# Layer 1's feed-forward in the form of layer 2: half blocks' products, down sums by row block, and the next layer's modulation on VectorE

## The chip, the cores and the metric

One core of a Trainium2 chip runs the whole kernel. The metric is the device time of one execution in microseconds (us). The core has five engines with an instruction list each, which each works through in its own order: TensorE (PE, matmuls), VectorE (DVE), ScalarE (ACT), GpSimd (POOL) and SyncE (SP, which here only issues DMA transfers; GpSimd issues some too).

## What is computed

Two layers of a backbone with 1024 latent and 256 context tokens of width 1024. The part that the change touches is the second half of layer 1 and the start of layer 2. `g2`, `sh2` and their like come from a modulation, a product of SiLU(c) with a 1024 x 6144 matrix per layer.

```
for i in range(DEPTH):                                  # 2 layers
    mod = (s_lat @ w_mod[i] + b_mod[i])[:, None, :]     # latents; mod_c the same from s_ctx, for the context
    sh1, sc1, g1, sh2, sc2, g2 = jnp.split(mod, 6, axis=-1)
    h = rms_norm(x, norm_mix[i]) * (1.0 + sc1) + sh1
    y, yc = token_mixers(h, hc, ...)
    x = x + g1 * y
    h = rms_norm(x, norm_ffn[i]) * (1.0 + sc2) + sh2
    x = x + g2 * swiglu(h, w_gate[i], w_up[i], w_down[i])   # 1024 -> 2816 -> 1024
    if need_ctx_out:                                    # layer 1 alone: the same for the context, xc
        ...
return rms_norm(x, final_norm)
def swiglu(h, w_gate, w_up, w_down):
    return (jax.nn.silu(h @ w_gate) * (h @ w_up)) @ w_down
```

All is float32. A product of two float32 operands is made from three matmuls of rounded operands: high by high, high by low and low by high part. Layer 1 is `l == 0` in the code, layer 2 `l == 1`.

## The kernel before

Tokens lie along the free axis, features on the 128 partitions: `x[k]` holds 128 features of 1280 tokens, latents in the blocks `B0` and `B1` of 512 and the context in `BC` of 256. `split` (lines 230 to 235) makes the two parts of a weight: ScalarE rounds the high one (L232), VectorE subtracts for the low one (L234), in a pool `wx` of eight buffers that also holds other tiles. A weight arrives in one of two buffers `wr` by a DMA of SyncE.

**Layer 1's FFN** is `ffn`. For each of 22 groups `f` of 128 hidden features it loads a column block of gate and up and a row block of down, and for each of the three token blocks it makes gate and up (`pg`, `pu`, 24 matmuls each, L441), the hidden value `a`, its parts `ah` and `al`, and then for each of the 8 output row blocks `m` three matmuls into `pd` (L1156), which VectorE adds at once into `x[m]` with the gate as factor (L1157). So VectorE takes 528 results out of PSUM. `last_norm` is the context's norm, which runs beside the first group. The squares for the next norm come with the last `f` (`add`), and layer 2's norm (`norm_block`) runs from there, block by block, beside layer 2's first projections, as the jobs in `pending`.

**Layer 2's modulation** is made meanwhile by `modulation_aside`: twelve units of 512 columns, each the sum of eight row blocks of `w_mod` times a scalar per partition, for latents and context (`v`). GpSimd multiplies and adds (L345, L346, `macc`), SyncE loads (`wm`), VectorE transposes and sums each unit (L351, L352), and four matmuls and an addition at the end turn it into `modT`. A merge draws two of its steps for three of `ffn`'s.

**Layer 2's FFN** has another form already. `out_proj` writes x to DRAM (`xmD`), since the norm then takes its place. `gates_seven` takes the 1024 latents as two halves of tokens and the 1024 features as two halves of rows, pairs the groups `f` and makes each 2 x 2 block product from seven products of half blocks in place of eight, with sums and differences of operands: `token_sums` makes those of the tokens once (`t1` to `t4`), `weights` those of the weights on GpSimd. The first four jobs (`early`) have their first two products drawn ahead of the token sums, as these need the norm and time. The hidden value goes to DRAM, `aD`. Then `down_blocks` loads the hidden features of 512 tokens (`hidden`: a load through GpSimd's queue and a split each, `ha`), and per output row block `m` three weights (1024, 1024 and 768 rows) give 66 matmuls into one `pd` (L1379), which VectorE adds to `xm` (L1398).

**What sets the order.** The program is written as above and given to a scheduler that works with a model of the engines (`schedule_with_timeline_sim`): it may put an engine's instructions in another order than they are written in, while the buffers of a pool go to the tiles in the order of the code. Each engine then runs its list as it stands, and an instruction that waits holds all behind it on its engine.

Of the kernel before, what the change touches and what calls it, by code (L numbers as in the profile page):

```python
# [11 lines left out]
F32 = mybir.dt.float32  # L12
# [75 lines left out]
def hybrid_layers(ctx: ExitStack, tc: tile.TileContext, A, K, out):  # L88
# [105 lines left out]
    xmD = [dr.tile([128, T], F32, name=f"xmD{k}") for k in range(KD)]  # L194
    aD = [dr.tile([128, T], F32, name=f"aD{f}") for f in range(NF)]
# [132 lines left out]

    def halves(t):
        return [t[:, 0:512], t[:, 512:1024]]  # L330

    def modulation_aside(l, u0, u1, part, sums, select):
        nu = u1 - u0
        pv4 = part[:, 0:32 * nu].rearrange("p (v b) -> p v b", v=2)
        for u in range(u0, u1):
            acc = sums()
            for k in range(KD):
                r = t_p("wm")[:, 0:512]
                SY.dma_start(r, A["w_mod"][l, 128 * k:128 * k + 128, 512 * u:512 * u + 512])
                for v in range(2):  # L340
                    if k == 0:
                        G.tensor_scalar(acc[v], r, sT[:, k, v:v + 1], None, ALU.mult)
                        continue
                    t = t_ev("mp")
                    G.tensor_scalar(t, r, sT[:, k, v:v + 1], None, ALU.mult)  # L345
                    G.tensor_tensor(acc[v], acc[v], t, ALU.add)  # L346
                if k % 2:
                    yield
            for v in range(2):
                t = t_ev("mtr")  # L350
                V.transpose(t, acc[v])  # L351
                V.tensor_reduce(pv4[:, v, 16 * (u - u0):16 * (u - u0) + 16], t.rearrange("p (b c) -> p b c", c=32),  # L352
                                axis=AX.X, op=ALU.add)
            yield
        sel = select()
        G.memset(sel, 0.0)
        for g in range(4):
            r = slice(32 * g, 32 * g + 32)
            V.tensor_copy(rev(sel[r], 0, [[160, 4], [1, 32]]), ident[r, r].unsqueeze(1).to_broadcast([32, 4, 32]))
        tp = p_c("modt")  # L360
        for q in range(4):
            PE.matmul(tp[:, 0:8 * nu], sel[:, 128 * q:128 * q + 128],
                      part[:, 0:32 * nu].rearrange("p (m q) -> p q m", q=4)[:, q], start=(q == 0), stop=(q == 3))
        V.tensor_tensor(modT[l][:, :, 4 * u0:4 * u1], tp[:, 0:8 * nu].rearrange("p (v j) -> p v j", v=2),
                        bmT[:, 48 * l + 4 * u0:48 * l + 4 * u1].unsqueeze(1).to_broadcast([128, 2, 4 * nu]), ALU.add)
        for w in range(2):
            if u0 <= 6 * w + 3 < u1:
                mod_vectors(l, w)
        yield


# [116 lines left out]
    def gla(l, hh, hl, ctx_out, before, given):  # L488
# [8 lines left out]
        def gproj(items, put, with_ctx, given=()):  # L497
            given = list(given)
            w = given + [None] * (len(items) - len(given))
            for blk in blks:  # L500
# [570 lines left out]
    def out_proj(l, blks):  # L1071
# [9 lines left out]
        def part(grp):  # L1081
# [6 lines left out]
            for m in range(KD):  # L1088
                w = wcols(A["w_out"][l], 128 * m)
                for o, n in grp:  # L1090
# [6 lines left out]
                    if len(blks) == 2:  # L1097
                        G.dma_start(xmD[m][:, o:o + n], x[m][:, o:o + n])
# [3 lines left out]
        def norms():  # L1102
            for blk in blks[:-1]:
                rs = block_rstd(ss, blk)
                yield
                r = rs()
                for k in range(KD):
                    xv, pool = x[k][:, blk[0]:blk[0] + blk[1]], k % 2 == 1
                    if len(blks) == 2:
                        scaled(l, xv, r, k, yh, yl, blk)  # L1110
                    else:
                        modulate(l, 1, xv, r[:, :blk[1]], k, yh, yl, blk, pool)
                    yield
        run(merge(part(blks[-1:]), norms(), 1, 2))
        rs = block_rstd(ss, blks[-1])
        if len(blks) == 2:
# [483 lines left out]
```

## Time and profile before

| | us |
|---|---|
| median of 3 runs (range) | 3234.38 (3233.16 to 3243.77) |
| the profiled execution | 3235.02 |
| its span, first to last instruction | 3233.2 |
| layer 1's FFN, first matmul to the last start of a down matmul | 886.7 to 1826.0 |
| layer 2's half-block products | 2514.8 to 2960.5 |
| layer 2's down sums and the final norm | 2962.1 to 3233.2 |

The span's mean granted clock of TensorE is 0.972 of full speed. A row that counts instructions as x528 has 528 of them in the group; a window's row gives for each engine the busy time and, in brackets, the number of instructions. Matmuls overlap in TensorE, so the distance between two starts is the price of one, and not the duration that its row shows.

### The profile page before, as it was taken

The page shows a single profiled execution, that of the slowest core. Times are in us where ns is not written, and L with a number is a line of the kernel's source. Part 1 is how long each engine was busy: PE and PEld are TensorE (multiplying, and loading weights), DVE is VectorE, ACT ScalarE, POOL GpSimd, SP SyncE. Part 2 cuts the span into 40 slices and gives each one's busy share as a digit, 9 for nine tenths or more (in the row PEclk, how much of TensorE's full clock was granted, in tenths as well). Part 3 has the DMA queues.
Part 4 walks back from the last instruction along what each step waited for, and adds up shares of the span by engine and source line. Part 5 has one row for each costly group of instructions (what it writes and reads, how often), then busy time and mean ns, then how long its engine had stood idle before and what let it go on. Part 6 is the DMA issues. An engine that isn't in the chain of part 4 may idle for free.

```text
span 3233.2 us, 50611 instructions
## 1 busy us (share of the span) xinstructions
PE 3067.4 (95%) x19726; PEld 2613.5 (81%) x19726; DVE 1726.4 (53%) x3431; ACT 1044.3 (32%) x1976; POOL 1087.8 (34%) x938
## 2 busy tenths in 40 slices
PE   7998999889999999999999899999989899999998
PEld 5887877677878888888888789887868688887877
DVE  3255444566675666666555724545766644444342
ACT  4332223455321111111111432224664444333231
POOL 1011020230189888887000101110411376655010
PEclk8999999999999999999999898999999999999999
DMA  7233455764312222222111223356555232225452
GB/s 251 84 125 104 126 160 156 209 186 155 92 62 72 82 79 82 79 82 66 40 40 38 76 66 98 95 155 184 148 172 171 69 101 79 79 85 170 143 187 80
DMA packets 371543, 365.80 MB, mean 113 GB/s; under 512 B 65100, under 2 KB 297512, under 8 KB 371304
## 3 DMA queue, kind: packets, MB, share of 16 engines
q1 hardware_dynamic: 358296, 318.79, 32.6%
q0 software_dynamic: 11856, 39.59, 3.8%
q10 hardware_dynamic: 1152, 4.19, 0.3%
q8 instruction: 155, 2.54, 0.3%
q14 instruction: 84, 0.69, 0.1%
HBM read 285.86 MB, written 76.64 MB: 112 GB/s over the span
## 4 chain that ended last, share of the span: by engine, by line
PE 72%; DMA 5%; DVE 4%; issue 3%; POOL 2%; ACT 1%; SPq 0%; DVEq 0%; ACTq 0%; POOLq 0%
PE q L1286 10%; PE pg L441 9%; PE pd L1156 9%; PE pu L441 9%; PE pd L1379 7%; PE op L441 6%; PE nqk L441 4%; PE ptp L849 3%; PE swp L448 2%; PE gp L441 1%; PE nao L863 1%; PE swo L863 1%; DMA wm<-in_w_mod_dram 1%; PE nvp L448 1%; PE gvp L448 1%
## 5 line engine op out<-in xcount | busy, mean ns | idle before, releaser
L1157 DVE SCALAR_TENSOR_TENSOR x<-pd,modT,x 128x512 f32<-128x512 f32 (+1 forms) x528 | 317.9, 655 | 195.0 <-PE pd L1156 192.9
L345 POOL TENSOR_SCALAR mp<-wm,sT 128x512 f32<-128x512 f32 x168 | 283.8, 1701 | 42.0 <-DVE mpart L352 35.9
L1286 PE MATMUL q<-yh,ws 128*128 128x512 f32 (+1 forms) x1056 | 282.9, 356 | 4.4 <-DVE us L1346 2.6
L1379 PE MATMUL pd<-ha,wdh 128*128 128x512 f32 (+1 forms) x748 | 225.2, 384 | 5.3 <-ACT ha L1170 2.2
L346 POOL TENSOR_TENSOR macc<-macc,mp 128x512 f32<-128x512 f32 x168 | 224.1, 1360 | 0.0
L830 ACT ACTIVATE P<-P,m 128x640 f32<-128x640 f32 (+2 forms) x216 | 167.2, 775 | 137.4 <-DVE m L826 131.4
L1286 PEld LDWEIGHTS q<-yh,ws 128*128 128x128 f32 x1056 | 183.3, 190 | 34.8 <-ACT ws L1170 5.6
L234 DVE TENSOR_TENSOR wcl<-wr,wch 128x1024 fp32r<-128x1024 f32 x98 | 140.7, 1435 | 124.1 <-ACT wch L232 122.5
L441 PE MATMUL pg<-yh,wch 128*128 128x512 f32 (+1 forms) x528 | 187.9, 356 | 1.0 <-ACT a L1146 1.0
L441 PE MATMUL pg<-yl,wch 128*128 128x512 f32 (+1 forms) x528 | 187.9, 356 | 0.0
L441 PE MATMUL pg<-yh,wcl 128*128 128x512 f32 (+1 forms) x528 | 187.4, 355 | 0.0
L441 PE MATMUL pu<-yl,wch 128*128 128x512 f32 (+1 forms) x528 | 187.1, 354 | 0.0
L441 PE MATMUL pu<-yh,wcl 128*128 128x512 f32 (+1 forms) x528 | 187.0, 354 | 0.0
L441 PE MATMUL pu<-yh,wch 128*128 128x512 f32 (+1 forms) x528 | 186.9, 354 | 0.0
L232 ACT ACTIVATE wch<-wr 128x1024 fp32r<-128x1024 f32 x100 | 106.0, 1060 | 245.3 <-PE pg L441 89.9
L1156 PE MATMUL pd<-al,wdh 128*128 128x512 f32 (+1 forms) x528 | 184.9, 357 | 0.0
L1156 PE MATMUL pd<-ah,wdl 128*128 128x512 f32 (+1 forms) x528 | 184.7, 357 | 0.0
L1286 PE MATMUL q<-yl,ws 128*128 128x512 f32 (+1 forms) x528 | 173.8, 356 | 0.4 <-DVE yl L1189 0.4
L1379 PEld LDWEIGHTS pd<-ha,wdh 128*128 128x128 f32 x748 | 139.9, 192 | 35.2 <-ACT ha L1170 3.8
L849 PE MATMUL ptp<-ident,P 128*128 128x128 f32 x984 | 144.5, 286 | 10.0 <-DVE pT L855 7.8
L1156 PE MATMUL pd<-ah,wdh 128*128 128x512 f32 (+1 forms) x528 | 148.6, 356 | 0.3 <-ACT ah L1149 0.3
L1379 PE MATMUL pd<-ha,wdl 128*128 128x512 f32 (+1 forms) x374 | 143.5, 384 | 0.8 <-DVE wdl L234 0.7
(351 smaller groups left out, 7809.9 us busy)
## 6 DMA issues: line engine op xcount, KB each, us to landing
wm<-in_w_mod_dram SPq DMA_DIRECT2D x96, 256.0 KB
wr<-in_w_gate_dram SPq DMA_DIRECT2D x46, 512.0 KB
wr<-in_w_up_dram SPq DMA_DIRECT2D x46, 512.0 KB
wm<-in_w_mod_dram POOLq DMA_DIRECT2D x32, 512.0 KB, 4.7
wr<-in_w_out_dram SPq DMA_DIRECT2D x32, 512.0 KB
wr<-in_w_down_dram SPq DMA_DIRECT2D x32, 512.0 KB
k<-naD SPq DMA_DIRECT2D x48, 320.0 KB
gm<-in_const_nam_dram SPq DMA_DIRECT2D x24, 576.0 KB
```

The lines of the kernel that those rows point to most:

```text
L232: S.activation(h, raw, AF.Copy)
L234: engine.tensor_tensor(l, raw, h.bitcast(F32), ALU.subtract)
L345: G.tensor_scalar(t, r, sT[:, k, v:v + 1], None, ALU.mult)
L346: G.tensor_tensor(acc[v], acc[v], t, ALU.add)
L441: PE.matmul(pt[:, :n], a[:, k, :], b[k][:, o:o + n], start=(k == 0 and i == 0), stop=(k == KD - 1 and i == 2))
L448: PE.matmul(pt[:, :n], a[k][:, t * 128:(t + 1) * 128], b[:, k % 2, c0:c0 + n], start=(k == 0 and i == 0), stop=(k == KD - 1 and i == 2))
L830: exps[:] = [S.activation(P, P, AF.Exp, bias=m[:, i:i + 1], scale=-1.0, accum_out=sums[:, i:i + 1])]
L849: line[:] = [PE.transpose(tp[:, (cc * 2 + i) * 128:(cc * 2 + i + 1) * 128], pr[i][:, (c + cc) * 128:(c + cc + 1) * 128], ident)]
L1156: PE.matmul(pd[:, :n], w[:, m * 128:(m + 1) * 128], b[:, :n], start=(i == 0), stop=(i == 2))
L1157: V.scalar_tensor_tensor(x[m][:, o:o + n], pd[:, :n], modT[l][:, v, 40 + m:41 + m], x[m][:, o:o + n], ALU.mult, ALU.add)
L1286: PE.matmul(bank[:, n * c:n * c + n], wv[p], v, start=(start and k == 0 and q == 0), stop=(k == 3 and q == 2), skip_group_check=not start)
L1379: PE.matmul(pt[:, 0:n], w[i][:, f - f0, :], hs[f][b][:, c0:c0 + n], start=(f == 0 and q == 0), stop=(f == NF - 1 and q == 2))
```

## The change

It does five things.

1. `ffn` and `modulation_aside` go. `out_proj` writes x to DRAM in layer 1 too, context included, and puts the latents' norm in x's place by `scaled`.
2. `gates_seven` takes the context along (`ctx_too`): with a job's first products the weights of the halves `a11` and `a12` also multiply the context's normed tokens (`context`), and once more at the job's end with `a21` and `a22`; `context_done` makes the hidden value. `early` is three there, and the token sums `t2` lie elsewhere, since the context's tokens now fill the place that layer 2 uses.
3. `down_next` makes the down sums by row block for the two latent blocks and then for the context. Each block of sums is added to `xm`, written to DRAM for layer 2, squared on ScalarE and added to `ss` on VectorE.
4. The modulation moves from beside the gates to beside the down sums of the latents (`modulation_behind`, four steps for a row block) and from GpSimd to VectorE, which now multiplies and adds in one instruction; the first four units are made for latents and context, the other eight for one of them. Its loads go through GpSimd's queue into the pool `ev` of three buffers.
5. Layer 2's norm of the latents runs beside the context's down sums (`norms`, a step for every third draw), that of the context after them (`last_norm`), and layer 2's first projections take the blocks in the order B0, B1, BC.

```diff
@@ out_proj @@
-                    if len(blks) == 2:
-                        G.dma_start(xmD[m][:, o:o + n], x[m][:, o:o + n])
+                    G.dma_start(xmD[m][:, o:o + n], x[m][:, o:o + n])
...
@@ gates_seven @@
         def first_products(j, pa, pb):
-            product(0, pa, True)
-            product(1, pb, True)
+            w = product(0, pa, True)
+            if ctx_too:
+                bank = p_b("qc")
+                context(w, 0, bank)
+            w = product(1, pb, True)
+            if ctx_too:
+                context(w, 1, bank)
+                context_done(j, 0, bank)
...
+        def context(w, half, bank):
+            for k in range(4):
+                for q, (p, y) in enumerate(((0, yh), (0, yl), (1, yh))):
+                    PE.matmul(bank[:, 0:C], w[k][p], y[4 * half + k][:, T:N], start=(half == 0 and k == 0 and q == 0),
+                              stop=(half == 1 and k == 3 and q == 2))
...
@@ new: modulation_behind(l) @@
+        for u in range(12):
+            acc = t_x("macc", F32)
+            nv = 2 if u < 4 else 1
+            for k in range(KD):
+                r = t_ev("wm")
+                G.dma_start(r, A["w_mod"][l, 128 * k:128 * k + 128, 512 * u:512 * u + 512])
+                for v in range(nv):
+                    if k == 0:
+                        V.tensor_scalar(acc[:, v], r, sT[:, k, v:v + 1], None, ALU.mult)
+                    else:
+                        V.scalar_tensor_tensor(acc[:, v], r, sT[:, k, v:v + 1], acc[:, v], ALU.mult, ALU.add)
+                if k % 2:
+                    yield
+            for v in range(nv):
+                t = t_ev("mtr")
+                V.transpose(t, acc[:, v])
+                V.tensor_reduce(pv4[:, v, 16 * u:16 * u + 16], t.rearrange("p (b c) -> p b c", c=32),
+                                axis=AX.X, op=ALU.add)
+            yield
...
@@ new: down_next(l) @@
+        def sums(m, hs, n, pt):
+            for f0 in range(0, NF, KD):
+                nf = min(KD, NF - f0)
+                r = t_raw("wr", [128, KD, 128])
+                SY.dma_start(r[:, 0:nf], A["w_down"][l][128 * f0:128 * (f0 + nf), 128 * m:128 * m + 128]
+                             .rearrange("(k p) f -> p k f", p=128))
+                w = split(r[:, 0:nf], "wd", [128, nf, 128])
+                for f in range(f0, f0 + nf):
+                    for q, (i, b) in enumerate(((0, 0), (0, 1), (1, 0))):
+                        PE.matmul(pt[:, 0:n], w[i][:, f - f0, :], hs[f][b], start=(f == 0 and q == 0),
+                                  stop=(f == NF - 1 and q == 2))
...
+            for m in range(KD):
+                SY.dma_start(xs[m], xmD[m][:, o:o + n])
+                pt = either(p_a, p_b, "pd")
+                sums(m, hs, n, pt)
+                V.scalar_tensor_tensor(xs[m], pt[:, 0:n], modT[l][:, v, 40 + m:41 + m], xs[m], ALU.mult, ALU.add)
+                if blk != BC:
+                    SY.dma_start(xD[l + 1][:, m, o:o + n], xs[m])
+                if m == 0:
+                    S.activation(ss, xs[m], AF.Square)
+                else:
+                    sq = t_ev("sq")[:, 0:n]
+                    S.activation(sq, xs[m], AF.Square)
+                    V.tensor_tensor(ss, ss, sq, ALU.add)
+                for _ in range(4):
+                    next(aside, None)
...
@@ the driver @@
-        x, hh, hl, last_norm = out_proj(l, blks)
-        if not ctx_out:
-            gates_seven(l, x, hh, hl, last_norm)
+        x, hh, hl, rs = out_proj(l, blks)
+        gates_seven(l, x, hh, hl, rs, ctx_out)
+        if ctx_out:
+            hh, hl, last_norm = down_next(l)
+        else:
```

In the change's order of VectorE's instructions a row is line, operation, output and inputs, and the tile's size; "x2" stands for two alike in a row. The first piece is from layer 1's FFN in the kernel before: `pd` is a product of down, `macc` the modulation, `pu` the up product, `wcl` and `wch` the parts of a weight.

```order
L1157 SCALAR_TENSOR_TENSOR x_8278<-pd_9744,modT_113,x_8278 128x256
L1157 SCALAR_TENSOR_TENSOR x_8279<-pd_9749,modT_113,x_8279 128x256
L351 STREAM_TRANSPOSE mtr_10799<-macc_10429 128x512
L352 TENSOR_REDUCE mpart_9293<-mtr_10799 128x16
L351 STREAM_TRANSPOSE mtr_10802<-macc_10429 128x512
L1147 TENSOR_TENSOR a_9804<-a_9804,pu_9779 128x512
L352 TENSOR_REDUCE mpart_9293<-mtr_10802 128x16
L1150 TENSOR_TENSOR al_9808<-a_9804,ah_9807 128x512
L234 TENSOR_TENSOR wcl_9958<-wr_9954,wch_9956 128x1024
L1157 SCALAR_TENSOR_TENSOR x_8272<-pd_9811,modT_113,x_8272 128x512
```

Additions into x follow the matmuls one by one, with the modulation's transposes between them. Now VectorE's list in the down stage of layer 1, from the middle of the third latent row block on (lines are those of the changed kernel): `pd_14148` is the sum of that block (block 2, counting from 0), `wdl_14275` the low half of the first weights of block 3.

```order
L1331 SCALAR_TENSOR_TENSOR macc_14122<-wm_14139,sT,macc_14122 128x512
L1331 SCALAR_TENSOR_TENSOR macc_14122<-wm_14143,sT,macc_14122 128x512 x2
L1383 SCALAR_TENSOR_TENSOR xm_13896<-pd_14148,modT_113,xm_13896 128x512
L1391 TENSOR_TENSOR ss_13900<-ss_13900,sq_14235 128x512
L1331 SCALAR_TENSOR_TENSOR macc_14122<-wm_14238,sT,macc_14122 128x512 x2
L1331 SCALAR_TENSOR_TENSOR macc_14122<-wm_14242,sT,macc_14122 128x512 x2
L1336 STREAM_TRANSPOSE mtr_14246<-macc_14122 128x512
L1336 STREAM_TRANSPOSE mtr_14249<-macc_14122 128x512
L1337 TENSOR_REDUCE mpart_13990<-mtr_14246 128x16
L1337 TENSOR_REDUCE mpart_13990<-mtr_14249 128x16
L1329 TENSOR_SCALAR macc_14252<-wm_14253,sT 128x512 x2
L234 TENSOR_TENSOR wdl_14275<-wr_14271,wdh_14273 128x1024
```

There is one addition for a whole row block, and eleven more of VectorE's instructions stand between it and the next block's first weights. The second place is TensorE at the end of layer 1's FFN in the kernel before: `gp` is layer 2's first projection, over the context (`yh`, `yl` are its normed tokens), `ssb` and `rsb` the next block's norm, `pd` the last products of down.

```order
L441 MATMUL gp_17186<-yl_8271,wch_17182 128x256
L441 MATMUL gp_17186<-yh_8263,wcl_17184 128x256
L393 MATMUL ssb_16946<-ones,ss_16888 128x1 x4
L404 MATMUL rsb_17013<-ident,rbc_17011 128x128 x4
L1156 MATMUL pd_17056<-ah_17007,wdh_16653 128x512
L1156 MATMUL pd_17056<-al_17008,wdh_16653 128x512
L1156 MATMUL pd_17056<-ah_17007,wdl_16655 128x512
L1156 MATMUL pd_17071<-ah_17007,wdh_16653 128x512
```

There layer 2's projection over the context is drawn in among the last down products, and the norm's matmuls stand between. Now the end of the context's down sums: `hc` is the context's hidden value, `hh` and `hl` the latents' normed tokens.

```order
L1366 MATMUL pd_16746<-hc_15973,wdh_16809 128x256 x2
L1366 MATMUL pd_16746<-hc_15973,wdl_16811 128x256
L1366 MATMUL pd_16746<-hc_15973,wdh_16809 128x256 x2
L1366 MATMUL pd_16746<-hc_15973,wdl_16811 128x256
L397 MATMUL gp_16854<-hh_15982,wch_16850 128x512
L397 MATMUL gp_16854<-hl_15990,wch_16850 128x512
L397 MATMUL gp_16854<-hh_15982,wcl_16852 128x512
L397 MATMUL gp_16854<-hh_15983,wch_16850 128x512
```

The projection, over latents now, follows the last down product directly, with no matmul of a norm between.

## Rows read from the trace of the kernel before

**Rows 1.** The page's busy line: engine, busy us, share of the span, instructions.

```profile
PE 3067.4 (95%) x19726; PEld 2613.5 (81%) x19726; DVE 1726.4 (53%) x3431; ACT 1044.3 (32%) x1976; POOL 1087.8 (34%) x938
```

**Rows 2.** Windows by stage: length, busy us PE PEld DVE ACT POOL, clock, DMA share, GB/s.

```profile
886.50:1810.00 923.50, 916.64 (x4782) 789.16 (x4781) 566.25 (x835) 158.10 (x235) 554.09 (x372) 1.00 0.20 64
2514.60:2961.50 446.90, 431.04 (x2126) 364.93 (x2124) 218.68 (x267) 180.10 (x310) 261.16 (x177) 0.98 0.27 84
2961.50:3233.20 271.70, 256.96 (x1186) 211.48 (x1186) 108.14 (x141) 79.59 (x122) 34.31 (x53) 0.96 0.47 150
```

**Rows 3.** Timeline of TensorE: start, duration, engine, line, operation, output and inputs.

```profile
1744.57 0.39 PE L441 MATMUL pg<-yh,wch 128*128 128x512 f32 x1
...
1750.01 0.39 PE L441 MATMUL pu<-yh,wch 128*128 128x512 f32 x1
...
1760.89 0.28 PE L441 MATMUL pg<-yh,wch 128*128 128x256 f32 x1
...
1763.04 0.28 PE L441 MATMUL pg<-yh,wch 128*128 128x256 f32 x1
```

**Rows 4.** Tiles pg, pd: count, ns least/median/most, first and last start, forms.

```profile
L441 PE MATMUL pg<-yh,wch x528: 277/389/792, 886.7 to 1791.2; 128*128 128x512 f32 x110, 128*128 128x256 f32 x66
...
L1156 PE MATMUL pd<-ah,wdl x528: 278/389/628, 907.9 to 1826.0; 128*128 128x512 f32 x110, 128*128 128x256 f32 x66
```

**Rows 5.** Tile q, the half blocks' products of layer 2.

```profile
L1286 PE MATMUL q<-yh,ws x1056: 277/389/632, 2514.8 to 2957.8; 128*128 128x512 f32 x111, 128*128 128x256 f32 x65
...
L1286 PE MATMUL q<-t,ws x528: 388/389/797, 2547.3 to 2960.5; 128*128 128x512 f32 x176
```

**Rows 6.** Timeline of ScalarE: copies of a job's first product, fourteen jobs apart.

```profile
2617.72 0.60 ACT L1306 ACTIVATE p<-q 128x512 f32<-128x512 f32 x1 [0.94 <-PE q L1286]
...
2886.80 0.60 ACT L1306 ACTIVATE p<-q 128x512 f32<-128x512 f32 x1 [2.04 <-PE q L1286]
```

**Rows 7.** Windows within layer 2's half-block stage (first) and its down stage.

```profile
2550.00:2570.00 20.00, 14.26 (x62) 11.42 (x61) 14.94 (x25) 6.73 (x11) 6.64 (x5) 0.78 0.26 79
2961.00:2980.00 19.00, 15.49 (x49) 10.83 (x50) 12.15 (x13) 7.33 (x13) 13.43 (x16) 0.82 0.72 245
3000.00:3050.00 50.00, 50.00 (x222) 41.41 (x221) 16.02 (x16) 10.81 (x11) 0.00 (x0) 1.00 0.42 126
3110.00:3130.00 20.00, 17.78 (x66) 13.90 (x66) 9.28 (x13) 5.05 (x9) 2.18 (x3) 0.83 0.88 280
```

**Rows 8.** Groups by line and form on VectorE: busy us, mean ns, idle before.

```profile
L234 DVE TENSOR_TENSOR wdl<-wr,wdh 128x1024 fp32r<-128x1024 f32 x32 | 39.2, 1224 | 50.6 <-ACT wdh L232 49.7
...
L383 DVE TENSOR_TENSOR ss<-ss,sq 128x512 f32<-128x512 f32 x42 | 28.8, 686 | 1.0
...
L351 DVE STREAM_TRANSPOSE mtr<-macc 128x512 f32<-128x512 f32 x24 | 16.8, 701 | 0.0
...
L352 DVE TENSOR_REDUCE mpart<-mtr 128x16 f32<-128x512 f32 x24 | 16.0, 677 | 0.4
...
L419 DVE TENSOR_SCALAR nt<-nt,av,modT 128x512 f32<-128x512 f32 x16 | 13.4, 840 | 0.4 <-ACT yh L418 0.3
...
L1398 DVE SCALAR_TENSOR_TENSOR xm<-pd,modT,xm 128x512 f32<-128x512 f32 x15 | 11.2, 750 | 28.2 <-PE pd L1379 27.9 <-DMA xm<-xmD 0.3
```

**Rows 9.** Timeline of ScalarE and VectorE near the start of layer 2's half-block stage.

```profile
2510.68 0.63 ACT L382 ACTIVATE sq<-x 128x512 f32<-128x512 f32 x1 [0.20 <-ACT ws L1170]
...
2527.91 2.74 DVE L1187 SCALAR_TENSOR_TENSOR x<-x,av,rs 128x512 f32<-128x512 f32 x4 [1.45 <-ACT rs L406]
```

**Rows 10.** DMA issues of GpSimd's queue: count, KB each, median us to landing.

```profile
ar<-aD POOLq DMA_DIRECT2D x44, 256.0 KB, 5.1
...
xmD<-x POOLq DMA_DIRECT2D x16, 256.0 KB, 2.4
```

**Rows 11.** Timeline of ScalarE in layer 2's down stage: two high halves of weights.

```profile
3004.24 1.06 ACT L232 ACTIVATE wdh<-wr 128x1024 fp32r<-128x1024 f32 x1 [1.69 <-DVE wdl L234]
3007.87 1.06 ACT L232 ACTIVATE wdh<-wr 128x1024 fp32r<-128x1024 f32 x1 [2.56 <-DMA wr<-in_w_down_dram]
```

More of the change, by code (lines that the diff above doesn't have):

```diff
@@ L325, in modulation @@
             yield
[L329 to L369, printed above, removed]
     def square_sums(x, blks):
@@ L499, in gproj @@
             w = given + [None] * (len(items) - len(given))
-            for blk in blks:
+            for blk in blks if l == 0 else (B0, B1, BC):
                 for i, (c0, ctx_too) in enumerate(items):
@@ L1209, in token_sums @@
         for k in range(4):
-            t1, v22 = half(x[k], 0), half(x[k + 4], 1)
+            t1, v22, v21 = half(x[k], 0), half(x[k + 4], 1), half(x[k + 4], 0)
             V.tensor_tensor(t1, v22, t1, ALU.subtract)
+            if ctx_too:
+                V.tensor_tensor(v21, v21, t1, ALU.subtract)
+                ops["t2"][k] = whole(t_s("t2", F32R) if k else t_x("t2"))
+                parts(t1, b2[k], ops["t2"][k])
+                continue
             j = 2 * k
@@ L1273, in gates_seven, with take @@
         ready = [next(feed) for _ in range(3)]
-        def product(i, bank, start):
-            w, b = ready.pop(0), ops[order[i]]
+        def take():
+            w = ready.pop(0)
             new = next(feed, None)
@@ L1279, in product @@
                 ready.append(new)
+            return [[t.rearrange("p (k f) -> p k f", f=128)[:, k] for t in w] for k in range(4)]
+        def product(i, bank, start):
+            w, b = take(), ops[order[i]]
             for k in range(4):
-                wv = [t.rearrange("p (k f) -> p k f", f=128)[:, k] for t in w]
                 for q, (p, m) in enumerate(((0, 0), (0, 1), (1, 0))):
@@ L1322, in gates_seven @@
         next(sums)
[L1323 removed]
+        if early == 4:
+            held[3] = first_products(3, p_b("q1"), p_b("q2"))
         run(sums)
@@ L1347, in gates_seven, with modulation_behind @@
             done(j, 1)
-            product(6, pd, False)
+            if ctx_too:
+                bank = p_b("qc")
+                context(take(), 0, bank)
+            w = product(6, pd, False)
+            if ctx_too:
+                context(w, 1, bank)
+                context_done(j, 1, bank)
             V.tensor_tensor(result(j, 2), u2, pd, ALU.add)
             done(j, 2)
+    def modulation_behind(l):
+        part = wk.tile([128, 7, 64], F32, tag="sx", name=nm("mpart"), bufs=2).rearrange("p a b -> p (a b)")[:, 0:384]
+        V.memset(part, 0.0)
+        pv4 = part.rearrange("p (v b) -> p v b", v=2)
+        for u in range(12):
[17 more added lines that the diff above has]
+            yield
+        sel = t_ev("sel")
+        V.memset(sel, 0.0)
+        for g in range(4):
+            r = slice(32 * g, 32 * g + 32)
+            V.tensor_copy(rev(sel[r], 0, [[160, 4], [1, 32]]), ident[r, r].unsqueeze(1).to_broadcast([32, 4, 32]))
+        tp = p_c("modt")
+        for q in range(4):
+            PE.matmul(tp[:, 0:96], sel[:, 128 * q:128 * q + 128],
+                      part.rearrange("p (m q) -> p q m", q=4)[:, q], start=(q == 0), stop=(q == 3))
+        V.tensor_tensor(modT[l][:, :, 0:48], tp[:, 0:96].rearrange("p (v j) -> p v j", v=2),
+                        bmT[:, 48 * l:48 * l + 48].unsqueeze(1).to_broadcast([128, 2, 48]), ALU.add)
+        for w in range(2):
+            mod_vectors(l, w)
+        yield
@@ L1354, in down_blocks, with norms_first @@
+    def norms_first(gen):
+        for i, _ in enumerate(gen):
+            yield
+            yield
+            yield
     def down_blocks(l, gain):
```

160 lines of the change are left out of this document (80 added, 80 removed).

## The prediction

> **What bounds the kernel now.** I read the page's busy line first: TensorE is busy for 95% of the span [rows 1]. A busy share says nothing about a stage, so the windows by stage come next [rows 2]: in layer 1's FFN TensorE is busy for 916.6 of 923.5 us at a granted clock of 1.00, VectorE for 566 and GpSimd for 554. That stage ends when TensorE has issued its matmuls; nothing else sets it. The timeline gives the price of one: 24 matmuls of 512 columns start between 1744.57 and 1750.01, which is 5.44 / 24 = 0.2267 us each, and 18 of 256 columns between 1760.89 and 1763.04, 0.12 each [rows 3]. One f of 22 is 144 matmuls of 512 columns and 72 of 256: 144 x 0.2267 + 72 x 0.12 = 41.28, in all 908. The stage runs from 886.7 to 1826.0, 939.3 us [rows 4]; the 31 beyond 908 are its start, and its end with layer 2's first projections drawn into it.
>
> Layer 2 already runs the form that layer 1 gets, so its rows carry the estimate: half blocks' products from 2514.8 to 2960.5 [rows 5], at 19.22 us a job once they run (14 jobs from 2617.72 to 2886.80 by ScalarE's copy of a job's first product) [rows 6], then the down sums by row block.
>
> **The change, part by part.** Times are set against the profiled execution's 3235.0 us, 0.6 above the median of the three runs.
>
> 1. *Seven products for eight.* Gate and up over the latents take 2 x 2 x 24 x 22 = 2112 matmuls of 512 columns before and 22 x 7 x 12 = 1848 after; the context's and the down sums' numbers stay. 264 x 0.2267 = **-59.9 us**. The order of instructions has exactly 264 fewer matmuls.
>
> 2. *VectorE's additions into x and the modulation's place.* 528 evictions of down products become 24, and most of the 554 us of GpSimd work there goes. In the stage of before TensorE waits for neither [rows 2], so this gives nothing back: **0**.
>
> 3. *Both ends of the stage.* Layer 2's half-block stage needs 22 x 19.22 = 422.8 and lasts 445.7: 23 us are lost, most of them at its start while VectorE builds the token sums (busy 14.9 of the 20 us from 2550, TensorE 14.3) [rows 7]. Layer 1 has the context's products of three jobs in hand there (24 x 0.12 = 2.9 us a job), so I take 19. At the end TensorE goes straight from the context's last down product to projections whose norm is done (the order's second place): 2. Together 21 against 31: **-10** (-18 to +4, as the cover holds or not).
>
> 4. *Down sums begin.* In layer 2 the 19 us from 2961 hold 49 matmuls where 3000 to 3050 shows 4.44 a us, or 84: 35 x 0.2267 = 7.9 us [rows 7]. With the modulation's first loads among the `ha` loads: **+10** (5 to 15).
>
> 5. *Ten waits between row blocks.* This is what the change adds. VectorE's order in the down stage (first place of the order) puts, after block 2's eviction `xm<-pd_14148`, the `ss` addition, four `macc`, two transposes, two reduces and two `macc` of the next unit ahead of `wdl_14275`, the low half of block 3's first weights. VectorE runs its list in order, the eviction needs block 2's last matmul, and TensorE's list has block 3 directly behind block 2: after two matmuls it stands until that split is done. Number the 16 latent row blocks 0 to 15. The same holds from 1 to 2, 2 to 3, 3 to 4, 5 to 6, 6 to 7, 7 to 8, 10 to 11, 11 to 12, 12 to 13 and 13 to 14. At the other five changes the weights stand ahead. In layer 2's down of before nothing stands there, hence 4.44 matmuls a us.
>
> Prices: eviction 0.75, addition 0.69, transpose 0.70, reduce 0.68, weight split 1.22 [rows 8]; square on ScalarE 0.63 and `macc` 0.69 (four `x<-x,av,rs`, same kind and size, in 2.74) [rows 9]. With two handovers the addition ends 2.2 after the last matmul. The `macc` that starts a unit has one tensor operand: the nearest row, L419, reads 0.84, taken beside work of GpSimd [rows 8], so I take 0.6. The loads of w_mod now leave GpSimd's queue into three buffers, so several are issued only when a `macc` frees one. A 256 KB transfer of that queue takes 2.4 us (`xmD`, little else under way) or 5.1 (`ar`, five at once) [rows 10]. One to three are under way here: I take 3.5 and keep both ends.
>
> - 2 to 3: 2.2, four `macc` 5.0; the next load is issued there and lands at 8.5 (transposes and reduces, 2.8, fit beside); two starts 9.7; split **10.9**.
> - 1 to 2: two evictions, two transposes, addition 3.6; load 7.1; two starts, two `macc` 9.7; split **10.9**.
> - 3 to 4: 2.2; eight `macc`, the last four behind loads, 8.5; next load 12.0; two starts, split **14.4**.
> - 5 to 6: load issued at 1.5 lands at 5.0; `macc`, split **6.9**.
> - 6 to 7, 10 to 11, 11 to 12: no load in the way, **4.8** each.
> - 7 to 8: seven `ha` splits of the next half stand there too, 11.0, and a load: **12.5**.
> - 12 to 13: two `macc`, load 6.4, start, `macc`, split **8.9**.
> - 13 to 14: four `macc` (two behind loads) 7.2, load 9.9, start, `macc`, split **12.6**.
>
> Sum **+92**; with loads of 2.4 us it is 81, with 5.1 it is 108.
>
> What a rule would add: the Trainium skill's page "SBUF — State Buffer", section "SBUF: two separate sides", says that a DMA issued from GpSimd's queue waits for its descriptors while VectorE runs an instruction that takes both ports, a tensor_scalar among them, and gives 620 ns alone against 3100 beside one. That speaks against moving these loads and this work together. The 5.1 us of `ar`, issued between VectorE's splits, lean that way [rows 10]. By that rule alone, 2.5 us on the seven waits with a load would make the sum 110.
>
> 6. *The clock after a stop.* From 2961 to 2980 TensorE was idle for 3.5 us, but 7.9 us of matmuls are missing, at a granted clock of 0.82; from 3110 to 3130 idle 2.2, missing 23 x 0.2267 = 5.2, at 0.83; 2550 to 2570 shows 0.78 [rows 7]. So a stop costs 3 to 4.4 us beyond itself, spent at the lower of two levels. No row shows ten in turn: nothing as the one end, 44 as the other; I take 3 each: **+30**.
>
> 7. *The context's down sums.* Ideal 8 blocks of 66 x 0.12 = 7.9 us. Each block needs three weight loads through two buffers: in layer 2 a split that waits for its load starts 3.6 us after the one before [rows 11]; with its own 1.06 and the low half's 1.22 a buffer turns in 5.9, so there is a load every 2.95 us, and as the third is three quarters of the others, 8.5 a block: 8 x 0.6 = 5. VectorE has, per block, 3.4 of splits (2.75 x 1.22), 3.0 of the next norm (two parts of two instructions at 0.75) and 0.9 of sums at half size, 7.3, and stays below. Two broadcasts of the next norm's root, each a wait of TensorE for VectorE and ScalarE, add 4: **+9** (3 to 18).
>
> Sum: -59.9 + 0 - 10 + 10 + 92 + 30 + 9 = +71, so 3235 + 71 = **3306 us**.
>
> **Rivals.** *The stops are covered* (faster). Nine of the ten waits rest on where VectorE's weight split stands; if the split were in truth ready before the block ends, as in layer 2 [rows 7], terms 5 and 6 fall: 3235 - 51 = 3184. It decides from the mean stop: ten stops of 5.1 us with their clock would eat the 51 exactly. For it: in layer 2's down stage VectorE is busy for 16 of 50 us [rows 7]. Against it: an in-order list, in which the eviction of the finished block stands ahead of the split. *Short stops*: loads of 2.4 us or less, no clock loss, good ends: 3235 - 60 - 18 + 5 + 81 + 3 = 3246, and a little lower with cheaper VectorE work. *Loads on the path*: loads of 5.1 us or, by the skill's rule, slower still, with the clock's 44 and a context stage at 18: 3235 - 60 - 10 + 10 + 108 + 44 + 18 = 3345 and up to some 3380. *No fewer products* is excluded by the count in the order.
>
> **Numbers.** Forecast with its bounds, 3258 to 3362: 0.76. Stops covered, below 3225: 0.06. Short stops, 3225 to 3258: 0.08, half of it within 0.3%. Loads on the path, above 3362: 0.10. A measurement tells about 0.3%, 9.7 us. Faster 0.06, same 0.04, slower 0.90.
>
> **What would show it.** Term 1: 24.8 us (7 x 12 x 0.2267 + 48 x 0.12) between the gate evictions of two jobs. Term 5: in the latent down stage ten idle times of TensorE, each ended by `wdl` on VectorE or `wdh` on ScalarE, 5 to 14 us, and none at the other five changes; VectorE's rows there read eviction, `macc`, transpose, split. The stage would take some 239 + 130 us. Term 6: granted clock below 1 behind each. Term 3: no idle at layer 2's first projection. I am wrong if the latent down stage takes under 300 us, or if layer 2's unchanged parts move by more than 10.

## The result: slower by 2.6%, and the profile after

The changed kernel takes 3319.55 us (median of four runs, 3318.16 to 3330.94) against 3234.03 of before in the same sessions: the ratio is 1.0265, with a 95% interval of 1.0235 to 1.0295. The forecast was 3306, its range 3258 to 3362. The profiled execution of the changed kernel took 3319.68 us, 84.7 more than that of before.

The busy line of the page, to be read against [rows 1]:

```profile
PE 3049.2 (92%) x19462; PEld 2586.6 (78%) x19462; DVE 1668.7 (50%) x3274; ACT 1200.8 (36%) x2258; POOL 875.8 (26%) x931
```

There are 264 fewer matmuls, as counted ahead, and TensorE is busy for 18 us less; the span is 84 us longer all the same. The windows by stage say where (length, then busy us and instructions of PE, PEld, DVE, ACT, POOL, then granted clock, DMA share and GB/s): half blocks' products, down sums of the latents, down sums of the context, and layer 2 up to its own half-block stage.

```profile
882.80:1444.60 561.80, 552.84 (x2917) 475.02 (x2916) 268.13 (x317) 202.98 (x354) 254.52 (x180) 0.99 0.23 71
1444.60:1809.60 365.00, 273.63 (x1066) 215.76 (x1066) 207.37 (x287) 80.61 (x112) 86.07 (x156) 0.86 0.59 191
1809.60:1899.30 89.70, 78.41 (x554) 74.79 (x552) 62.73 (x100) 40.57 (x61) 13.72 (x25) 0.89 0.65 193
1899.30:2596.60 697.30, 659.36 (x5109) 571.89 (x5109) 357.86 (x960) 273.41 (x568) 89.62 (x131) 0.96 0.46 132
```

The first stage is what it was meant to be: full at a clock of 0.99. The second holds 16 row blocks of 66 matmuls, 16 x 66 x 0.2267 = 239.4 us at the price of [rows 3], and takes 365.0: 91.4 us in which TensorE stands idle, and 34 more that its matmuls took beyond their price, at a granted clock of 0.86. Part of both lies ahead of the first change that stops TensorE: from 1444.6 to 1485.5, 132 matmuls take 11.0 us over their price of 29.9.

```profile
1444.60:1485.50 40.90, 34.86 (x134) 26.00 (x133) 31.75 (x44) 13.63 (x21) 21.05 (x35) 0.92 0.96 325
```

Who ended the idle time there stands in TensorE's waits (us in total, times, longest):

```profile
PE pd L1366 <- DVE wdl L234: 50.3, 11, 10.6
PE pd L1366 <- ACT wdh L232: 27.8, 10, 5.3
PE ssb L349 <- DVE ss L1391: 7.6, 1, 7.6
PE pd L1366 <- DVE ha L1091: 3.0, 3, 1.1
PE pd L1366 <- ACT ha L1090: 2.5, 2, 1.9
```

85.7 of the 91.4 us are waits for a weight's high or low half, or for the sum of squares at the change of latent halves. All but 0.5 of them lie at exactly ten changes of row block, those ten that were named ahead, and none at the other five. The one from block 3 to 4 shows how they come about; here are TensorE's two rows that waited (others between them left out), and then VectorE's, ScalarE's and GpSimd's lists in that stretch (start, duration, engine, line, operation, output and inputs, and in brackets the idle time before and what ended it):

```profile
1541.87 0.73 PE L1366 MATMUL pd<-ha,wdh 128*128 128x512 f32 x2 [2.50 <-ACT wdh L232]
...
1553.22 0.80 PE L1366 MATMUL pd<-ha,wdl 128*128 128x512 f32 x1 [10.61 <-DVE wdl L234]
```

```profile
1539.41 0.75 DVE L1383 SCALAR_TENSOR_TENSOR xm<-pd,modT,xm 128x512 f32<-128x512 f32 x1 [10.49 <-PE pd L1366]
1540.91 0.69 DVE L1391 TENSOR_TENSOR ss<-ss,sq 128x512 f32<-128x512 f32 x1 [0.74 <-ACT sq L1390]
1541.52 2.73 DVE L1331 SCALAR_TENSOR_TENSOR macc<-wm,sT,macc 128x512 f32<-128x512 f32 x4
1544.87 1.42 DVE L1331 SCALAR_TENSOR_TENSOR macc<-wm,sT,macc 128x512 f32<-128x512 f32 x2 [0.62 <-DMA wm<-in_w_mod_dram]
1546.48 1.42 DVE L1331 SCALAR_TENSOR_TENSOR macc<-wm,sT,macc 128x512 f32<-128x512 f32 x2 [0.19 <-DMA wm<-in_w_mod_dram]
1547.81 1.30 DVE L1336 STREAM_TRANSPOSE mtr<-macc 128x512 f32<-128x512 f32 x2
1549.03 1.24 DVE L1337 TENSOR_REDUCE mpart<-mtr 128x16 f32<-128x512 f32 x2
1551.15 0.88 DVE L1329 TENSOR_SCALAR macc<-wm,sT 128x512 f32<-128x512 f32 x2 [0.89 <-DMA wm<-in_w_mod_dram]
1551.95 1.22 DVE L234 TENSOR_TENSOR wdl<-wr,wdh 128x1024 fp32r<-128x1024 f32 x1
```

```profile
1540.25 0.63 ACT L1390 ACTIVATE sq<-xm 128x512 f32<-128x512 f32 x1 [12.98 <-DVE xm L1383]
1540.78 1.99 ACT L232 ACTIVATE wdh<-wr 128x1024 fp32r<-128x1024 f32 x2
```

```profile
1541.89 0.54 POOL L1326 DMA_DIRECT2D wm<-in_w_mod_dram  x1 [12.14 <-DVE ss L1391]
1543.22 0.54 POOL L1326 DMA_DIRECT2D wm<-in_w_mod_dram  x1 [0.79 <-DVE macc L1331]
1548.19 0.54 POOL L1326 DMA_DIRECT2D wm<-in_w_mod_dram  x1 [4.43 <-DVE macc L1331]
```

This is to be read as a ring. VectorE idles for 10.49 us until block 3's last matmul (the eviction at 1539.41), because nothing that it may do stands ahead of the eviction. Behind it come the addition of squares, the rest of a unit of the modulation and the start of the next, and only then, at 1551.95, the split for which TensorE waits. GpSimd's row shows why the modulation's steps had not run in those 10.49 us: its next load of `w_mod` waited 12.14 us for `ss` on VectorE, that is for the buffer in which `sq` of the finished block lay.

### The profile page after: what moved, and what is told of

The parts are those of the page before. It is cut to its first block, busy times and chain, and to the rows that moved or that the text cites. A ratio compares the mean times of both kernels' runs of the same rounds, so it can differ in the third digit from the quotient of the medians.

```text
span 3317.6 us, 50944 instructions
## 1 busy us (share of the span) xinstructions
PE 3049.2 (92%) x19462; PEld 2586.6 (78%) x19462; DVE 1668.7 (50%) x3274; ACT 1200.8 (36%) x2258; POOL 875.8 (26%) x931
## 3 DMA queue, kind: packets, MB, share of 16 engines
q10 hardware_dynamic: 1152, 4.19, 0.3%
## 4 chain that ended last, share of the span: by engine, by line
PE 65%; DMA 7%; issue 6%; DVE 5%; POOL 2%; ACT 1%; SPq 0%; POOLq 0%; DVEq 0%; ACTq 0%
PE q L1217 22%; PE pd L1471 7%; PE op L397 6%; PE pd L1366 5%; PE nqk L397 4%; PE qc L1225 4%; PE ptp L805 3%; DMA wm<-in_w_mod_dram 3%; PE swp L404 2%; PE gp L397 2%; PE swo L819 2%; PE nao L819 1%; PE nvp L404 1%; DMA wr<-in_w_down_dram 1%; DMA ar<-aD 1%
## 5 line engine op out<-in xcount | busy, mean ns | idle before, releaser
L1217 PE MATMUL q<-yh,ws 128*128 128x512 f32 (+1 forms) x1760 | 515.6, 370 | 5.4 <-ACT gs L1248 2.0
L1217 PE MATMUL q<-t,ws 128*128 128x512 f32 x1320 | 320.6, 393 | 18.3 <-ACT t L1080 6.9
L1217 PEld LDWEIGHTS q<-t,ws 128*128 128x128 f32 x1320 | 247.6, 189 | 72.2 <-ACT t L1080 7.7
L1091 DVE TENSOR_TENSOR ws<-s,ws 128x512 fp32r<-128x512 f32 x176 | 180.6, 1027 | 181.1 <-ACT ws L1090 178.7
L1366 PE MATMUL pd<-ha,wdh 128*128 128x512 f32 x704 | 236.5, 419 | 33.4 <-ACT wdh L232 27.8
L1091 DVE TENSOR_TENSOR ws<-wr,ws 128x512 fp32r<-128x512 f32 x154 | 143.3, 935 | 193.7 <-ACT ws L1090 193.4
L1366 PEld LDWEIGHTS pd<-ha,wdh 128*128 128x128 f32 x704 | 143.6, 205 | 70.0 <-ACT wdh L232 31.7
L1366 PE MATMUL pd<-ha,wdl 128*128 128x512 f32 x352 | 148.9, 423 | 50.4 <-DVE wdl L234 50.3
L1217 PEld LDWEIGHTS q<-yl,ws 128*128 128x128 f32 x880 | 160.8, 190 | 25.1 <-DVE yl L1109 0.7
L1471 PEld LDWEIGHTS pd<-ha,wdh 128*128 128x128 f32 x748 | 139.8, 191 | 33.7 <-DVE ha L1091 2.8
L1225 PE MATMUL qc<-yh,ws 128*128 128x256 f32 x704 | 140.5, 283 | 0.0
```

The costliest lines, as they stand in the source:

```text
L1091: V.tensor_tensor(dst[1], v, dst[0].bitcast(F32), ALU.subtract)
L1217: PE.matmul(bank[:, n * c:n * c + n], w[k][p], v, start=(start and k == 0 and q == 0), stop=(k == 3 and q == 2), skip_group_check=not start)
L1225: PE.matmul(bank[:, 0:C], w[k][p], y[4 * half + k][:, T:N], start=(half == 0 and k == 0 and q == 0), stop=(half == 1 and k == 3 and q == 2))
L1366: PE.matmul(pt[:, 0:n], w[i][:, f - f0, :], hs[f][b], start=(f == 0 and q == 0), stop=(f == NF - 1 and q == 2))
L1471: PE.matmul(pt[:, 0:n], w[i][:, f - f0, :], hs[f][b][:, c0:c0 + n], start=(f == 0 and q == 0), stop=(f == NF - 1 and q == 2))
```

## Experiments

Theory A: the stops come from the place of the next block's weight split in VectorE's and ScalarE's lists, and that place from buffers. The weights wait for the buffer of `macc` (pool `wx`), `macc` for loads, a load for the buffer of `sq` (pool `ev`), and `sq` for the eviction. Rivals: the weights come late by themselves (B); the modulation's work and loads cost the time wherever they stand (C); the pool `wx` alone is the cause (D); GpSimd's queue delays the loads (E). The diffs show the lines that matter; "..." stands for code left out.

All kernels took the same 561.6 to 561.8 us for the half blocks' products. The part ahead of layer 1's FFN, the same in all, ended between 881.1 and 890.6 us in their profiled executions, so a few us between two totals say little, and the stages carry the argument.

### Without the modulation (e1_no_mod)

```diff
-        aside = modulation_behind(l + 1)
+        aside = iter(())
+        V.tensor_copy(modT[l + 1][:, :, 0:48], ...)      # the bias alone
...
```

> Left out: layer 2's modulation is not computed (its bias alone is used), so VectorE's products and additions of w_mod, their loads and the transposes are gone; the rest is the changed kernel. Theory A (the ten stops come from where VectorE's list has the next row block's first weights, and they stand behind the modulation's steps): no stop of over 2 us at any change of row block in the latent down stage, which takes 239 of matmuls + 10 at its start = 250 us where the changed kernel takes 365, clock back near 1; total 3320 - 115 = 3205. Rival B (the weights themselves arrive late through their two buffers, whatever VectorE does): stops stay at most changes, total above 3270.

Measured 3197.06 us, a ratio of 0.9882 (0.9868 to 0.9897) to before. The latent stage, and TensorE's waits in it:

```profile
1445.50:1691.20 245.70, 242.18 (x1066) 198.66 (x1065) 108.16 (x136) 83.07 (x117) 37.35 (x64) 1.00 0.57 183
```

```profile
PE pd L1366 <- DVE ha L1091: 2.8, 4, 1.1
PE pd L1366 <- DVE wdl L234: 0.7, 2, 0.5
```

No stop of over 1.1 us is left and the clock is at 1.00. So the weights arrive in time through two buffers (rival B falls). Of the 34 us that the matmuls took beyond their price 3 are left (245.7 - 239.4 - 3.5 idle), so the rest goes with the modulation and its stops. The new form of the FFN without the modulation would be faster than before; the modulation costs 122 us in it.

### The two links of the ring, one at a time and together (e2, e3, e4)

```diff
 e2, e4
-            acc = t_x("macc", F32)
+            acc = [p_c("macc") for _ in range(nv)]       # PSUM banks that lie idle here
...
 e3, e4
-                    sq = t_ev("sq")[:, 0:n]
+                    sq = t_w2("sq")[:, 0:n]
```

> The modulation's running sums macc lie in the free PSUM banks in place of the weights' pool wx; nothing else differs, and all of VectorE's work and loads of w_mod stay. In the order that results, the next block's first weights stand ahead of the eviction at all but none of the ten places. Theory A (place in the list): the latent down stage takes 250 to 260 us, total 3205 to 3215. Rival C (the work and the loads of the modulation cost the time by themselves, beside the down sums): at least half of the 85 us of stops and of the 34 us of clock stay, total above 3260.

> The squares sq of a finished row block take a buffer of the pool w2 in place of ev, which the loads of w_mod use; macc stays among the weights. In the order two of the ten places keep the weights behind the eviction (blocks 1 to 2 and 3 to 4, now with only two starts of a unit between). Theory A with its chain (weights wait for macc's buffer, macc for loads, loads for the buffer of sq, sq for the eviction): any link broken frees the rest, so two stops of some 5 to 8 us are left, the latent stage takes 265 to 275, total 3215 to 3230. Rival D (the pool wx alone is the cause): nearly all stops stay, 3300 or more.

> Both edits together. Theory A: no stop in the latent stage, 250 us, total 3205, no better than either edit that removes all ten. If the two act apart from each other, it is clearly faster than both.

Measured: 3226.38 us (0.9971 of before, 0.9957 to 0.9985), 3253.03 (1.0055, 1.0036 to 1.0075) and 3223.73 (0.9963, 0.995 to 0.9976). The latent stages of the three in this order:

```profile
1451.80:1721.40 269.60, 250.96 (x1067) 202.49 (x1065) 205.48 (x284) 81.01 (x111) 85.59 (x153) 0.97 0.79 254
```

```profile
1450.60:1747.30 296.70, 257.25 (x1082) 207.59 (x1080) 209.54 (x302) 80.49 (x110) 86.97 (x155) 0.94 0.73 235
```

```profile
1445.60:1717.10 271.50, 249.60 (x1082) 203.97 (x1080) 212.28 (x302) 81.61 (x111) 87.13 (x155) 0.96 0.81 257
```

VectorE does the same work as in the changed kernel (205 to 212 us against 207) in a stage that is 68 to 95 us shorter. So it is the place and not the work: rival C falls. Rival D, by which the pool `wx` alone is the cause, falls too, since moving only `sq` frees the weights at eight of the ten places. And both edits together give hardly more than the first. The windows of e3 and e4 hold 16 matmuls of the modulation's last step and of the next norm, which come after the context's first products in e2; from the first to the last start of a latent product it is 267.1 us in e2, 286.6 in e3 and 259.8 in e4. By the totals, the first edit takes 93 us off the changed kernel, the second 67 and both 96, while two separate causes would have added up to 160, more than the 122 that the whole modulation costs. That is what a ring does: opened at either place, it lets most of the time go.

All three totals missed the expectation, for a reason that it didn't name. In e2 TensorE still waits within the first block of the second latent half, 2.62 us for `ha`, 0.96 for `wdh` and 6.03 for `wdl`. In e4 it waits at the change between the latent halves, in e3 there and at the two places that the order left:

```profile
1580.18 1.87 PE L349 MATMUL ssb<-ones,ss 128*128 128x1 f32 x8 [6.31 <-DVE ss L1391]
1584.16 1.22 PE L1366 MATMUL pd<-ha,wdh 128*128 128x512 f32 x2 [2.12 <-ACT ha L1090]
```

```profile
1497.00 0.80 PE L1366 MATMUL pd<-ha,wdl 128*128 128x512 f32 x1 [6.01 <-DVE wdl L234]
...
1536.29 0.50 PE L1366 MATMUL pd<-ha,wdl 128*128 128x512 f32 x1 [4.16 <-DVE wdl L234]
...
1606.54 1.87 PE L349 MATMUL ssb<-ones,ss 128*128 128x1 f32 x8 [8.93 <-DVE ss L1391]
```

The first four units of the modulation (latents and context) are twice as heavy and all lie in the first latent half, whose end also brings 22 splits of hidden values; VectorE's list is crowded there. In e4 the list also errs the other way: TensorE is done with the block at 1573.87, but the eviction starts only at 1577.64, behind three `macc` that each waited for a load. Whether the crowding is it, e9 below tries.

### The loads issued by SyncE (e5_mod_loads_on_sync)

```diff
-                G.dma_start(r, A["w_mod"][l, 128 * k:128 * k + 128, 512 * u:512 * u + 512])
+                SY.dma_start(r, A["w_mod"][l, 128 * k:128 * k + 128, 512 * u:512 * u + 512])
```

> The loads of w_mod are issued by SyncE in place of GpSimd; all else is as in the changed kernel, and the ten places keep the next weights behind the eviction. Theory A (place in the list sets the stops, the loads land in 3.4 us whoever issues them): total within 6 us of the changed kernel's 3320. Rival E (loads from GpSimd's queue are held up while VectorE works, as the prediction weighed): the stops with a load in their way shrink by 1 to 2 us each, total 3303 to 3312. Rival F (on SyncE's list a waiting load of w_mod holds the loads of weights behind it): total above 3326.

Measured 3334.57 us (ratio 1.03, 1.0283 to 1.0317), 15 more than the changed kernel. The latent stage:

```profile
1450.30:1829.50 379.20, 275.05 (x1066) 216.16 (x1065) 206.53 (x284) 79.53 (x111) 33.94 (x57) 0.84 0.57 183
```

It is 14 us longer, as rival F had it (on SyncE's list a waiting load of `w_mod` holds up the weights behind it); theory A had put the total within 6 us of the changed kernel's. That the longer stage comes from weights' loads held up behind a waiting load on SyncE's list is argued from the order and not shown apart. In the changed kernel nothing shows that GpSimd's queue delayed the loads: all 96 issues took 0.54 to 0.59 us on GpSimd (shortest, median and longest in ns in the first row), whatever VectorE did beside them, and a load landed 3.4 us after its issue (the median, in the second):

```profile
L1326 POOL DMA_DIRECT2D wm<-in_w_mod_dram x96: 536/537/593, 1455.9 to 1804.0; - x96
```

```profile
wm<-in_w_mod_dram POOLq DMA_DIRECT2D x96, 256.0 KB, 3.4
```

### The context's down sums (e6, e7)

The stage holds 8 x 66 x 0.12 = 63.4 us of matmuls and took 89.4 from its first to its last matmul. Either the weights' loads through two buffers hold it (theory G) or the next norms beside it (rival H).

```diff
 e6
-        rq = block(BC, hs, xs, norms_first(norms()))
+        rq = block(BC, hs, xs, iter(()))
+        run(norms())
 e7
...
-                r = t_raw("wr", [128, KD, 128])
+                if n == C and turns[0] % 2 == 0:
+                    r = spare[turns[0] // 2 % 2][:, 0:1024]...
+                else:
+                    r = t_raw("wr", [128, KD, 128])
```

> The next layer's norms of the latents run behind the context's down sums in place of beside them; nothing else differs. It costs some 40 to 60 us of its own, so the stage is what counts: the context's down sums take 89 us in the changed kernel, of which 64 are matmuls at full clock. Theory G (each row block's three weights come through two buffers, and their loads hold the stage): 80 to 88 us remain. Rival H (VectorE's and ScalarE's work on the norms holds it): 66 to 72 us.

> In the context's down sums every second weight is loaded into one of two further buffers (tiles that lie idle there), so four loads can be under way; the rest is the changed kernel. Theory G (loads through two buffers): the stage falls from 89 to 68 to 76 us and its granted clock rises, total 3303 to 3308. Rival H (norm work): 85 us or more, total 3316 to 3322.

Without norms beside it the stage takes 82.9 us (total 3337.26, ratio 1.031):

```profile
1820.50:1903.40 82.90, 73.01 (x544) 68.84 (x543) 41.48 (x67) 29.18 (x42) 5.26 (x9) 0.96 0.54 158
```

With four buffers it takes 83.5 (total 3313.92, ratio 1.0234, 1.0218 to 1.0249), where theory G had 68 to 76, and the total lies 6 us above its expectation. But the two stages lose in different places. With four buffers the last 58 us are full at a clock of 1.00. Here they are, then the last 60 of the changed kernel and the last 58 of the one without norms beside:

```profile
1836.00:1894.00 58.00, 57.55 (x471) 56.55 (x471) 48.58 (x66) 33.00 (x45) 6.97 (x13) 1.00 0.77 227
```

```profile
1839.00:1899.20 60.20, 53.59 (x396) 51.53 (x394) 39.57 (x54) 26.86 (x37) 4.28 (x8) 0.91 0.60 176
```

```profile
1845.30:1903.50 58.20, 52.75 (x414) 50.40 (x414) 26.00 (x32) 20.19 (x26) 0.00 (x0) 1.00 0.54 155
```

That is 8.1 us for a block of 66 with four buffers, 10.0 in the changed kernel and 9.3 without the norms. So the two buffers were the main bound of the steady part (theory G), and the norms beside them had a smaller share. What four buffers gained there was partly lost ahead of it: the stage's first 25.6 us hold only 57 of its 528 products, with one long wait that is new:

```profile
1827.22 0.80 PE L1372 MATMUL pd<-hc,wdh 128*128 128x256 f32 x2 [8.85 <-ACT wdh L232]
```

On ScalarE's list the high half of the second weight had come to stand behind all 22 splits of the context's hidden values, the last of which waited for its load:

```profile
1825.80 0.42 ACT L1090 ACTIVATE hc<-ar 128x256 fp32r<-128x256 f32 x1 [1.64 <-DMA ar<-aD]
1826.13 1.77 ACT L232 ACTIVATE wdh<-wr 128x1024 fp32r<-128x1024 f32 x2
```

It is the same kind of stop, at another place.

### Put together (e8, e9, e10)

e8 joins e2 and e7. e9 also spreads the heavy units of the modulation and draws a weight one ahead. e10 is e9 with the squares in `w2`.

```diff
 e9, e10
-        for u in range(12):
+        for u in (0, 4, 5, 1, 6, 7, 2, 8, 9, 3, 10, 11):
...
```

> Running sums in PSUM and four weight buffers for the context together. If the two are apart from each other, 3226 (measured with the sums in PSUM) less what the four buffers give alone: 3210 to 3214; by rival H 3226.

> Running sums in PSUM, the four heavy units of the modulation (latents and context) spread among the eight light ones in place of ahead of them, weights of a row block drawn one ahead, and two further weight buffers for the context. With the sums in PSUM alone the latent stage lost 31 us, 12 of it at the change between the two latent halves, where VectorE's list was crowded, and the rest at its start and in the clock. Theory A (what is left is crowding of the list by the heavy units): 15 to 22 us lost in the latent stage, total 3205 to 3215. If the crowding is not it: 3220 as before this edit.

> As the mixed kernel, with the squares in the pool w2 too. In the order the last latent sums come before the loads of the context's hidden values are split, so ScalarE and VectorE have all 22 splits behind them: the change to the context costs 5 to 10 us more and the latent stage 3 to 5 less; total 3208 to 3222.

Measured: 3222.78 us (0.9954, 0.9939 to 0.9969), **3213.39** (0.9924, 0.991 to 0.9937, median of six) and 3222.32 (0.9947, 0.9934 to 0.996). e9 beats both kernels, that of before by 0.8%. Its latent stage, and TensorE's waits there:

```profile
1447.00:1701.00 254.00, 245.86 (x1066) 199.13 (x1064) 200.57 (x271) 77.67 (x104) 78.79 (x140) 0.99 0.81 262
```

```profile
PE pd L1380 <- DVE ha L1091: 6.7, 7, 1.8
PE pd L1380 <- ACT ha L1090: 0.6, 1, 0.6
PE pd L1380 <- DVE wdl L234: 0.5, 2, 0.3
PE ssb L349 <- DVE ss L1405: 0.2, 1, 0.2
```

All of the modulation now fits beside the latents' sums for 254.0 - 245.7 = 8 us over a stage without it. As e9 changes the order of the units and the draw of the weights at once, it doesn't show which of the two took the last stops away.

e8 missed its expectation by some 9 us. That had been set before e7 was measured; with the 5.6 us that four buffers gave alone, 3226.4 - 5.6 = 3220.8, the two edits do add up within 2 us. What is left are waits behind a change of stage, of 3.35 and 5.54 us in the first block of the second latent half and of 4.19, 3.59 and 5.03 at the start of the context. e10 came out 0.3 us above its range, and by another way than expected: its latent stage got longer than e9's, not shorter (with the 16 further matmuls as in e4), while the context's stage, at 86.0 us for 92.4, got shorter. Here are e10's latent stage and, in it, TensorE's wait of 15.13 us at the change of halves for the first split on ScalarE:

```profile
1442.80:1711.60 268.80, 247.55 (x1082) 202.78 (x1081) 211.12 (x294) 80.34 (x107) 81.45 (x146) 0.97 0.80 257
```

```profile
1584.30 0.79 PE L1380 MATMUL pd<-ha,wdh 128*128 128x512 f32 x1 [15.13 <-ACT ha L1090]
```

In e9 the context's stage still loses: it takes 92.4 us, with all waits of over 0.9 us in its first 33. That is open for another step.

## Why the prediction was right

The direction, the mechanism and its ten places came out as forecast; the sum, +71, was 14 us short of the 84.7 between the two profiled executions.

1. *Seven products* (-59.9) and the start of term 3 (19 us): forecast 22 x 24.8 + 19 = 564.6, measured 561.8. The job time is read off ScalarE's copies, twelve jobs apart, (1298.31 - 999.75) / 12 = 24.88:

```profile
999.75 0.60 ACT L1256 ACTIVATE p<-q 128x512 f32<-128x512 f32 x1 [2.06 <-PE q L1217]
...
1298.31 0.60 ACT L1256 ACTIVATE p<-q 128x512 f32<-128x512 f32 x1 [2.06 <-PE q L1217]
```

2. *VectorE's freed work* (0): right as far as the first stage goes. VectorE is busy for 268 of 562 us there and TensorE for 553, so its work did not bound the stage.

3. *Both ends* (-10): the start was right, the end was mis-sized. 48 matmuls of layer 2's projections over the context ran within the FFN's end before; I counted their time as lost and gave it back. They now run later, 48 x 0.12 = 5.8 us, and TensorE idles 0.95 and 0.53 us at the first projection, whose weight is still being split. That is most of the 9 us by which layer 2 up to its half-block stage got longer (697.7 from the last start of a down product, against 688.8). The sign that TensorE would not idle there failed with it.

4. *The start of the down sums* (+10): right. It is the 11.0 us from 1444.6 to 1485.5; without the modulation the whole latent stage lost 6.3.

5. *Ten waits* (+92): TensorE's idle times at the ten places are, from 1 to 2 on, 8.6, 9.5, 13.1, 6.2, 3.7, 16.5, 3.3, 3.7, 8.5 and 12.1, together 85.2, where I had 10.9, 10.9, 14.4, 6.9, 4.8, 12.5, 4.8, 4.8, 8.9 and 12.6. Loads landed in 3.4 us, where 3.5 was taken; a `macc` took 0.75 for 0.69, the one that starts a unit 0.49 for 0.6. Six of the ten lie in the 5 to 14 us that were named as the sign. Two details were wrong. The first part of a stop, about 2.5 us, ends with ScalarE's high half, which stands behind `sq` on ScalarE's list: TensorE doesn't even start the block, and I had let two of its matmuls run. And at the change of halves (16.5 for 12.5) the norm's `ssb` waits 7.6 us for `ss` on TensorE's list ahead of the next block, which the working left out. The rule of the Trainium skill's page "SBUF — State Buffer", section "SBUF: two separate sides", by which a DMA from GpSimd's queue is held up while VectorE runs an instruction that takes both ports, would have put the sum at 110, an estimate from the page's figures. This trace does not bear it out: all 96 issues took 0.54 to 0.59 us, those during which VectorE ran a `tensor_scalar` (from 1611.2 and from 1719.9) among them, and the sum is smaller.

6. *The clock* (+30): what is left of the 125.6 us over the price, behind the start's 11.0 and the stops' 85.2, is 29.4. The experiment without stops shows 1.00, so it comes with the stops.

7. *The context's down sums* (+9, 3 to 18): the stage is 26 us over its matmuls. This is the term that was mis-sized. The cause was named, three loads through two buffers, but the load every 2.95 us was too short: from 1839 on 396 matmuls, six blocks, took 60.2 us, 10.0 a block for the 8.5 that I took (2.95 us a load, with the third at three quarters, would even make 8.1). That is 9 of the 17 us. The other 8 lie in the first two blocks, which took 29.4 us for some 21 with the 4 us of the norm's broadcasts. I gave the clock no share in this stage, while it stood at 0.83 there and at 0.91 behind:

```profile
1809.60:1839.00 29.40, 24.72 (x160) 23.25 (x159) 23.16 (x47) 13.61 (x24) 9.44 (x17) 0.83 0.74 227
```

Measured less forecast: -3 in the first stage; +1 at the start of the down sums, -7 in the stops and about 0 in the clock; +17 in the context's stage and +7 behind it. The rest, -4 ahead of the FFN, -1 in layer 2's half-block stage and +3 in its down stage, lies in parts that the change hardly touches. So the total lies closer than its terms: 24 us too little at the end stand against some 9 too much before it. The rival of covered stops fell with the first row of waits, and the one with loads on the path was not needed.

## What to carry to other kernels

Where work is moved beside a stage that is bound by TensorE, look at what will stand between the last result of one tile and the operands of the next on each engine that prepares them. Free time on that engine does not help if its list has the eviction first. Here the order was made by buffers: if the moved work and the next operands, or the moved work's loads and a result that hangs on the eviction, draw from one pool, the ring closes, and a buffer elsewhere for either opens it. Before work is moved to an engine with time to spare, read the order of that engine's list.

## What the runs showed that was not expected

A stop costs more than itself: 85 us of stops took some 29 us of clock with them. And the steady part of the context's sums, 57.55 of 58 us busy, ran at 1.00 with four buffers, while the same loop with two buffers and gaps of up to 2.8 us showed 0.91. And up to the start of layer 1's FFN, where all kernels run the same matmuls, single executions differ by 9.5 us (881.1 to 890.6), so that a total of one execution says less than a stage.
